# The low-part product of the attention logits over all 128 rows of the array

## The chip, the cores and the metric

The kernel runs on one core of a Trainium2 chip. The core has five engines that work side by side, each through its own instructions in order: TensorE (PE; its weight loads are shown apart as PEld), VectorE (DVE), ScalarE (ACT), GpSimd (POOL) and SyncE (SP), which here only issues DMAs. They share an on-chip memory of 128 partitions; PE writes into eight banks of a second memory (PSUM), which DVE and ACT read. The metric is the device time of one execution in microseconds (us).

## The reference, cut to what matters

One decoder block on 512 tokens of width 1024: a token-mixing half (attention with 8 heads of 64, beside a pooling branch) and a feed-forward half of width 2816. All in float32.

```
h = rms_norm(x) * (1 + scale1(c)) + shift1(c)
q, k, v, p, g_attn, g_pool = split(h @ W_in)
q, k = rms_norm(q per head), rms_norm(k per head)
logits = q k^T * 64^-0.5 + bias(distance), causal
attn = softmax(logits) v
pool = (trailing window mean of p - p) @ pool_w * pool_scale
merged = sigmoid(g_attn) * (attn @ Wa) + sigmoid(g_pool) * (pool @ Wp)
x = x + gate1(c) * (merged @ W_out)
u = causal_conv3((rms_norm(x) * (1 + scale2(c)) + shift2(c)) @ W_up)
x = x + gate2(c) * ((silu(u_g) * u_v) @ W_down)
```

With 512 tokens in blocks of 256, each query's own block and the one past block are all selected, so the block-sparse attention is plain causal attention.

## The kernel before

PE multiplies in a reduced form of float32 (fp32r). To keep accuracy each operand is split into a high part (rounded to that form) and a low part (what is left), and a product is made of three passes: high x high, high x low, low x high (`mm3`, lines 117 to 120). ACT makes most of the high parts, DVE the low parts.

The stages follow each other on PE: q and p projections while h is still being made, then k, then v, then eight heads of attention woven into the sixteen units of the two gate projections, then the branch merge, the output projection, the up projection with convolution, and the down projection. Weights come in units of 128x1024 (512 KB) by DMAs from SP, as many at a time as there are buffers (`wraw`, 5), two units ahead of their use (`ahead`, `unit`).

The order of PE, DVE and ACT is the order in which the code is written: generators (`tok_proj`, `gate_proj`) yield after each step of three passes, and `fill` (line 350) takes as many steps as a number of microseconds says before it lets the next piece of attention in. POOL takes the reciprocal square roots (`pow`), the low part of one q unit and of W_out, and issues the DMAs of the bias rows (`trev`).

The logits of a head have only 64 channels, half the array. So the two halves of the 128 partitions are put to use (`stacks`, from line 387): Q of a head is a tile of 128 rows whose one half holds the high part of q and whose other half the low part; K1 holds the high part of k in both halves. One 128-row product Q x K1 gives (q_hi + q_lo) k_hi. What is missing, q_hi k_lo, is a product over 64 rows, with K2: the low part of k in the same half in which Q holds q_hi. One tile K2 serves a pair of heads, the even head's low part in rows 0 to 63 and the odd head's in rows 64 to 127, and the low product reads one half of it and of Q:

```
K1[h], K2[h] = k1, k2[a]                                            # line 410
half = slice((h % 2) * 64, (h % 2) * 64 + 64)                       # line 422
nc.tensor.matmul(sps[:, :n], Q[h][half, tslice(qt)], K2[h][:, :n], start=True, stop=False)   # line 431
nc.tensor.matmul(sps[:, :n], Q[h][:, tslice(qt)], K1[h][:, :n], start=False, stop=True)      # line 432
```

`logits(h)` does so for four query tiles, the last first, over n = 512, 384, 256 and 256 keys: eight products, 64-row and 128-row in turn. DVE then adds the bias and takes the maximum of each row (line 440), ACT the exponential (line 444), DVE normalizes (line 454). `flip(h)` transposes the probabilities on PE (line 467), ACT and DVE split them, and `values(h)` multiplies by v (line 481); ACT copies half of the result (`bot`, line 488) and DVE adds (line 489). The loop over heads (lines 596 to 614) writes: flip(h), logits(h + 1), softmax(h + 1), some gate steps, the stacks of a later pair, values(h), a modulation column or two (`ada_col`, line 181), gate steps. Head 0's logits stand in the v projection (line 571). When a gate unit is done, ACT copies it out of its bank (line 347).

The tiles Q, K1, K2, the bias rows, probabilities and most others are slots of one pool of 72 (`slot`, line 66).

Of the kernel before, what the change touches and what calls it, by code (L numbers as in the profile page):

```python
# [7 lines left out]
F32 = mybir.dt.float32  # L8
F32R = mybir.dt.float32r
# [6 lines left out]
P = 128  # L16
# [10 lines left out]
BIG = 1e30  # L27
# [4 lines left out]
ET = mybir.EngineType  # L32
ENG = {ET.PE, ET.DVE, ET.Activation}

# columns of the constant pack
C_N1 = 0
C_N2 = C_N1 + 8
C_QG = C_N2 + 8
# [10 lines left out]
def block_kernel(tc, x, cvec, ada, wtok, wch, pool_w, wbr, wout, wup, wdn, pack, table, out):  # L49
    nc = tc.nc  # L50
# [3 lines left out]
    with ctx:  # L54
# [11 lines left out]
        def slot(name, dt=F32, w=512):  # L66
            return sp.tile([P, w], dt, tag="s", name=name)
# [6 lines left out]
            nc.sync.dma_start(raw, src)  # L74
            return raw

        # weight units in the order the tensor engine takes them
        plan = []
        for i in range(4):
            plan += [(wtok[12 + i], f"p{i}"), (wtok[i], f"q{i}")]  # L80
# [19 lines left out]
            return hi  # L100

        def ahead(name, n=2, on_dve=False, pool=()):
            """Emits loads and splits up to n units past the named one."""
            while upto[0] < min(len(plan), pos[name] + n + 1):
                src, nm = plan[upto[0]]
                raw = early.pop(nm) if nm in early else load_unit(src, nm)
                hi = his.pop(nm) if nm in his else hi_of(nm, raw, on_dve)
                lo = wlo_p.tile([P, 1024], F32R, tag="lo", name=f"lo_{nm}")
                (nc.gpsimd if nm in pool else nc.vector).tensor_sub(lo, raw, hi.bitcast(F32))  # L109
                ready[nm] = (hi, lo)  # L110
                upto[0] += 1
# [8 lines left out]
            nc.tensor.matmul(ps, sl, mh, start=False, stop=stop)  # L120

        def mm3s(ops, start, stop, late=0):
            """The three passes of several products, pass by pass; late: the moving low part comes last."""
            for ps, sh, sl, mh, ml in ops:
                nc.tensor.matmul(ps, sh, mh, start=start, stop=False)
            for i in ((1, 0) if late else (0, 1)):
                for ps, sh, sl, mh, ml in ops:
                    nc.tensor.matmul(ps, sl if i else sh, mh if i else ml, start=False, stop=stop and i != late)  # L128

        tslice = lambda t: slice(t * P, (t + 1) * P)  # L130

# [1 line left out]
        pk = cpool.tile([P, C_END], F32, name="pk")  # L133
        ident = pk[:, C_ID : C_ID + P]
        col = lambda i: pk[:, i : i + 1]
# [9 lines left out]
        nc.vector.memset(mhalf, -0.5)  # L145
        acol = cpool.tile([P, 48], F32, name="acol")

# [1 line left out]
        xt = []  # L149
        for t in range(TT):  # L150
            row = []
# [4 lines left out]
            xt.append(row)  # L156

        def rms_rows(tiles, name):
            """1 / rms per token of two [128, 512] halves of a token tile."""
            ss = mini.tile([P, 2], F32, tag="ss", name=f"ss_{name}")  # L160
            for f in range(2):
                junk = slot(f"junk_{name}_{f}")
                if f == 0:
                    nc.scalar.activation(junk, tiles[f], AF.Square, scale=1.0 / math.sqrt(D), accum_out=ss[:, f : f + 1])
                else:
                    nc.vector.tensor_tensor_reduce(
                        out=junk, in0=tiles[f], in1=tiles[f], op0=ALU.mult, op1=ALU.add, scale=1.0 / D,
                        scalar=EPS, accum_out=ss[:, f : f + 1])
            ms = mini.tile([P, 1], F32, tag="ms", name=f"ms_{name}")
            nc.vector.tensor_add(ms, ss[:, 0:1], ss[:, 1:2])  # L170
            rs = mini.tile([P, 1], F32, tag="rs", name=f"rs_{name}")
            nc.gpsimd.tensor_tensor(rs, ms, mhalf[:, 0:1], op=ALU.pow)
            return rs

# [1 line left out]
        def ada_load(g, k):  # L176
            return load_unit(ada[g * 8 + k], f"ada_{g * 8 + k}")

# [15 lines left out]
            (eng or nc.vector).tensor_sub(lo[:, :w], src, hi[:, :w].bitcast(F32))  # L194
            return hi, lo

# [1 line left out]
        fd = dpool.tile([H, NF], F32, name="fd")  # L198

        def bias_table():  # L200
# [38 lines left out]
            else:  # L239
                nc.vector.tensor_scalar(xs[k], xT[k], col(C_N1 + k), None, op0=ALU.mult)  # L240

        # loads of the first phase: modulation rows and weights, as many at a time as there are buffers
        queue = [(0, 0), (1, 0), "p0", "q0", (0, 1), (1, 1), (0, 2), (1, 2), "p1", "q1", (0, 3), (1, 3),
                 (0, 4), (1, 4), (0, 5), (1, 5), "p2", "q2", (0, 6), (1, 6), (0, 7), (1, 7), "p3", "q3"]
        held = [0]
# [30 lines left out]
        def lo_h(k):  # L276
            nc.vector.tensor_sub(hl[k], xs[k], hh[k].bitcast(F32))

# [1 line left out]
        pump()  # L280
        sum_h(0)
        gs = mini.tile([P, 1], F32, tag="gs", name="gs")
# [16 lines left out]
        for k in range(KT):  # L299
            i = k // 2  # L300
# [54 lines left out]
                us -= c  # L355

        def head_sums(ps, name):
            """1 / rms over each head's 64 columns of the token-major tiles."""
            res = []
            for t in range(TT):  # L360
                sq = slot(f"sq_{name}_{t}")
                nc.scalar.activation(sq, ps[t], AF.Square)
                ss = mini.tile([P, H], F32, tag="hs", name=f"hs_{name}_{t}")
                nc.vector.tensor_reduce(ss, sq.rearrange("p (h d) -> p h d", d=64), axis=AX.X, op=ALU.add)
                nc.vector.tensor_scalar(ss, ss, 1.0 / 64, EPS, op0=ALU.mult, op1=ALU.add)
                rs = mini.tile([P, H], F32, tag="hr", name=f"hr_{name}_{t}")
                nc.gpsimd.tensor_tensor(rs, ss, mhalf, op=ALU.pow)
                res.append(rs)
            return res
# [11 lines left out]
        qgn = cpool.tile([P, 1], F32, name="qgn")  # L381
        nc.vector.tensor_scalar(qgn, col(C_QG), -0.125, None, op0=ALU.mult)

# [1 line left out]
        Q, K1, K2 = {}, {}, {}  # L385

        def stacks(pr, isq):
            src, gain = (qn, qgn) if isq else (kn, col(C_KG))
            tp = bank(f"T_{pr}_{isq}")
            for t in range(TT):  # L390
                nc.tensor.transpose(tp[:, tslice(t)], src[t][:, tslice(pr)], ident)
            for e in range(2):
                h = 2 * pr + e
                a = slice(e * 64, e * 64 + 64)
                b = slice(64 - e * 64, 128 - e * 64)
                if isq:
                    q = slot(f"Q_{h}", F32R)
                    nc.scalar.activation(q[a], tp[a], AF.Copy, scale=gain[a])
                    nc.vector.scalar_tensor_tensor(
                        q[b], tp[a], gain[a], q[a].bitcast(F32), op0=ALU.mult, op1=ALU.subtract)  # L400
                    Q[h] = q
                else:
                    k1 = slot(f"K1_{h}", F32R)
                    if e == 0:
                        k2 = slot(f"K2_{pr}", F32R)
                    for r in (a, b):
                        nc.scalar.activation(k1[r], tp[a], AF.Copy, scale=gain[a])
                    nc.vector.scalar_tensor_tensor(
                        k2[a], tp[a], gain[a], k1[a].bitcast(F32), op0=ALU.mult, op1=ALU.subtract)
                    K1[h], K2[h] = k1, k2[a]  # L410

        ath, atl = [], []
        apair = {}

        def logits(h):
            """exp of head h's logits less their maximum: four query tiles over their causal keys."""
            trev = slot(f"trev_{h}")
            fsrc = fd[h : h + 1, :]
            nc.gpsimd.dma_start(
                trev, bass.AP(tensor=fsrc.tensor, offset=fsrc.offset, ap=[[1, P], [1, 512]]))  # L420
            ta = trev[:, :]
            half = slice((h % 2) * 64, (h % 2) * 64 + 64)
            pss = []
            for qt in (3, 2, 1, 0):
                n = max((qt + 1) * P, 256)
                if qt:
                    sb = bank(f"S_{h}_{qt}")
                    sps = sb
                else:
                    sps = sb[:, 256:]  # L430
                nc.tensor.matmul(sps[:, :n], Q[h][half, tslice(qt)], K2[h][:, :n], start=True, stop=False)  # L431
                nc.tensor.matmul(sps[:, :n], Q[h][:, tslice(qt)], K1[h][:, :n], start=False, stop=True)  # L432
                pss.append(sps)
            rows, sms = [], []
            for i, qt in enumerate((3, 2, 1, 0)):
                n = (qt + 1) * P
# [4 lines left out]
                    out=L[:, :n], in0=pss[i][:, :n], in1=rev, op0=ALU.add, op1=ALU.min, scale=1.0,  # L441
# [12 lines left out]
                nc.vector.tensor_scalar(rows[i][:, :n], rows[i][:, :n], ri, None, op0=ALU.mult)  # L454
            return rows[::-1]

        # P^T: key tile on the partitions; key tile kt holds queries kt*128 ..
        place = {0: (0, 0), 1: (1, 0), 3: (1, 384), 2: (2, 0)}

        def flip(h, rows):  # L460
# [31 lines left out]
                ath.append(a)  # L492
                atl.append(b)

# [1 line left out]
        plh, pll, pls = {}, {}, {}  # L496
        pwh = slot("pwh", F32R)
        pwl = slot("pwl", F32R)
# [25 lines left out]
                tl, ps2, col(C_PS + g), th.bitcast(F32), op0=ALU.mult, op1=ALU.subtract)  # L524
            plh[g], pll[g] = th, tl

# [1 line left out]
        praw = []  # L528
        for g in range(4):
            pt = slot(f"pt_{g}")  # L530
# [24 lines left out]
        fill(kgen, 2)  # L555
        fill(kgen, 100)

# [1 line left out]
        kr = head_sums(kps, "k")  # L559
        vps = [bank(f"v_{t}") for t in range(TT)]  # L560
        vgen = tok_proj(2, vps, "v")
# [9 lines left out]
        rows = logits(0)  # L571
        fill(vgen, 2)
        rows = softmax(0, *rows)
# [9 lines left out]
                nc.vector.tensor_sub(dst[:, :, 1], src, dst[:, :, 0].bitcast(F32))  # L583
            vst.append(vt)

# [1 line left out]
        gates = {}  # L587

        def gate_stream():
# [24 lines left out]
            fill(gg, (share - 3) / 2)  # L614
        fill(gg, 1000)

# [1 line left out]
        def row_of(g, name):  # L618
            rows = []
            for f in range(2):  # L620
# [36 lines left out]
            ada_col(4, k)  # L657
        late = [KT - 2, KT - 1]

# [1 line left out]
        wsel = lambda k, f: wo[(k // 2) * 4 + f * 2 + k % 2]  # L661
        x2, xr = [], {}
        h2h = [slot(f"h2h_{k}", F32R) for k in range(KT)]
# [63 lines left out]
                out_post(3, 0, ops[3, 0])  # L727
                flip_h2(1)

# [1 line left out]
        yh, yl = [], []  # L731

        def conv(ps, i, name):
# [41 lines left out]
            if 4 <= j < 12:  # L775
                ada_col(5, j - 4)

# [1 line left out]
        g2 = row_of(5, "g2")  # L779
        NK = NP // 2  # L780
        for f in range(2):
# [99 lines left out]
```

## Time and profile before

| | |
|---|---|
| median of 3 runs | 704.27 us (704.16 to 704.55) |
| span of the profiled execution, from first to last instruction | 702.0 us |
| what lies around the span (704.27 - 702.0) | 2.3 us |
| instructions in the profile | 8487 |
| DMA: 94.50 MB, mean | 135 GB/s |

The profile gives no separate time for the execution it was taken from; the median of the runs less its span is taken as what lies around it. Times in the profile's rows count from the span's start. In a timeline's row stand the start in us, the duration in us, the engine, the line, the operation, the tile written and the tiles read, the shapes, the count, and in brackets how long the engine had been idle and what ended that. For PE the shape 64*128 is the stationary operand (rows of the array by columns), and 64x512 the moving one (rows by columns). A PE row's duration reaches to a modelled end and overlaps the next row: distances are read from start to start. The tile names in rows leave the numbers out: S is a head's logits, PT its transposed probabilities, O its values product.

### The profile page before, as it was taken

How to read it: one execution, taken by the hardware profiler on the slowest of the kernel's cores; microseconds unless marked ns; L12 is line 12 of the kernel's file. 1: busy time of each engine (PE TensorE's matmuls, PEld its weight loads, DVE VectorE, ACT ScalarE, POOL GpSimd, SP SyncE). 2: the span in 40 equal slices, each digit the busy share in tenths (PEclk: the TensorE clock that was granted, in tenths of full speed). 3: DMA queues.
4: the chain of work that ended last, by engine and by line, in shares of the span. 5: the costliest groups of instructions: out<-in, count | busy, mean ns of one | idle time of the engine just before them, and what ended most of it. 6: DMA issues, size and time to landing. Idle time of an engine off the chain costs nothing.

```text
span 702.0 us, 8487 instructions
## 1 busy us (share of the span) xinstructions
PE 690.7 (98%) x3238; PEld 568.9 (81%) x3238; DVE 443.7 (63%) x719; ACT 304.8 (43%) x490; POOL 57.6 (8%) x56
## 2 busy tenths in 40 slices
PE   6999999999999999999999999999999999999997
PEld 4788787777777888888988888888888888888886
DVE  5795876776777598876576676776655653225213
ACT  6554447555554565504654343453443433122110
POOL 2103040000000045601000000000000000000000
PEclk9999999999999999999999999999999999999999
DMA  8785241544442356681123434534323233324001
GB/s 313 267 350 180 71 141 38 165 132 146 151 136 93 102 187 207 196 312 60 62 69 112 150 122 149 158 115 148 97 83 120 66 114 123 116 91 151 31 1 60
DMA packets 27631, 94.50 MB, mean 135 GB/s; under 512 B 3283, under 2 KB 3708, under 8 KB 27590
## 3 DMA queue, kind: packets, MB, share of 16 engines
q1 hardware_dynamic: 26198, 89.63, 37.7%
q0 software_dynamic: 1392, 4.33, 2.2%
q8 instruction: 25, 0.41, 0.2%
q14 instruction: 16, 0.13, 0.0%
HBM read 91.83 MB, written 2.12 MB: 134 GB/s over the span
## 4 chain that ended last, share of the span: by engine, by line
PE 95%; ACT 2%; DVE 1%; issue 1%; DMA 1%; SPq 0%; POOL 0%; DVEq 0%
PE u L118 11%; PE u L119 11%; PE u L120 11%; PE d L119 6%; PE d L118 6%; PE d L120 6%; PE gate_ps L120 4%; PE gate_ps L119 4%; PE gate_ps L118 4%; PE o L120 2%; PE o L118 2%; PE o L119 2%; PE S L432 2%; PE S L431 2%; PE O L481 1%; PE p L128 1%
## 5 line engine op out<-in xcount | busy, mean ns | idle before, releaser
L118 PE MATMUL u<-h2h,hi_up 128*128 128x512 f32 (+1 forms) x384 | 142.7, 372 | 0.0
L119 PE MATMUL u<-h2l,hi_up 128*128 128x512 f32 (+1 forms) x384 | 142.6, 371 | 0.0
L120 PE MATMUL u<-h2h,lo_up 128*128 128x512 f32 (+1 forms) x384 | 142.6, 371 | 0.0
L120 PEld LDWEIGHTS u<-h2h,lo_up 128*128 128x128 f32 x384 | 72.3, 188 | 12.6
L118 PEld LDWEIGHTS u<-h2h,hi_up 128*128 128x128 f32 x384 | 72.3, 188 | 12.5
L119 PEld LDWEIGHTS u<-h2l,hi_up 128*128 128x128 f32 x384 | 72.3, 188 | 12.3
L118 PE MATMUL d<-hi_dn,y_h 128*128 128x512 f32 (+1 forms) x198 | 72.6, 367 | 0.0
L119 PE MATMUL d<-lo_dn,y_h 128*128 128x512 f32 (+1 forms) x198 | 72.6, 367 | 0.0
L120 PE MATMUL d<-hi_dn,y_l 128*128 128x512 f32 (+1 forms) x198 | 72.4, 365 | 0.0
L109 DVE TENSOR_TENSOR lo_dn<-raw_dn,hi_dn 128x1024 fp32r<-128x1024 f32 x22 | 26.6, 1224 | 61.6 <-ACT hi_dn L99 61.6
L181 DVE CUSTOM_DVE_ANT_0 raw_ada<-raw_ada,cbc 128x1026 f32<-128x1026 f32 x48 | 61.1, 1293 | 3.0 <-DMA raw_ada<-in_ada 3.0
L109 DVE TENSOR_TENSOR lo_up<-raw_up,hi_up 128x1024 fp32r<-128x1024 f32 x44 | 52.1, 1221 | 8.6 <-ACT hi_up L99 8.6
L99 ACT ACTIVATE hi_dn<-raw_dn 128x1024 fp32r<-128x1024 f32 x22 | 23.0, 1059 | 75.0 <-PE d L120 61.7
L736 ACT ACTIVATE uv<-u,pk 128x512 f32<-128x512 f32 x22 | 17.2, 780 | 87.1 <-PE u L120 87.1
L120 PE MATMUL gate_ps<-h_h,lo_gate 128*128 128x512 f32 x128 | 50.0, 390 | 0.0
L119 PE MATMUL gate_ps<-h_l,hi_gate 128*128 128x512 f32 x128 | 49.9, 390 | 0.0
L118 PE MATMUL gate_ps<-h_h,hi_gate 128*128 128x512 f32 x128 | 49.9, 390 | 0.0
L737 DVE SCALAR_TENSOR_TENSOR uv<-u,pk,uv 128x511 f32<-128x511 f32 x22 | 16.5, 749 | 52.5 <-ACT uv L736 52.5
L99 ACT ACTIVATE hi_up<-raw_up 128x1024 fp32r<-128x1024 f32 x44 | 44.1, 1046 | 4.3 <-PE u L119 4.3
L118 PEld LDWEIGHTS d<-hi_dn,y_h 128*128 128x128 f32 x198 | 37.4, 189 | 6.3
L119 PEld LDWEIGHTS d<-lo_dn,y_h 128*128 128x128 f32 x198 | 37.3, 189 | 6.1
L120 PEld LDWEIGHTS d<-hi_dn,y_l 128*128 128x128 f32 x198 | 37.3, 188 | 6.1
(201 smaller groups left out, 1241.0 us busy)
## 6 DMA issues: line engine op xcount, KB each, us to landing
raw_ada<-in_ada SPq DMA_DIRECT2D x48, 513.0 KB, 4.8
raw_up<-in_wup SPq DMA_DIRECT2D x44, 512.0 KB, 4.3
raw_dn<-in_wdn SPq DMA_DIRECT2D x22, 512.0 KB, 3.4
raw_gate<-in_wch SPq DMA_DIRECT2D x16, 512.0 KB, 5.3
raw_br<-in_wbr SPq DMA_DIRECT2D x8, 512.0 KB, 3.8
raw_wo<-in_wout SPq DMA_DIRECT2D x8, 512.0 KB, 3.2
x<-in_x SPq DMA_DIRECT2D x8, 256.0 KB, 4.4
raw_p<-in_wtok SPq DMA_DIRECT2D x4, 512.0 KB, 5.9
```

What stands on the lines that cost most here:

```text
L99: nc.scalar.activation(hi, raw, AF.Copy)
L109: (nc.gpsimd if nm in pool else nc.vector).tensor_sub(lo, raw, hi.bitcast(F32))
L118: nc.tensor.matmul(ps, sh, mh, start=start, stop=False)
L119: nc.tensor.matmul(ps, sh, ml, start=False, stop=False)
L120: nc.tensor.matmul(ps, sl, mh, start=False, stop=stop)
L128: nc.tensor.matmul(ps, sl if i else sh, mh if i else ml, start=False, stop=stop and i != late)
L181: nc.vector.tensor_tensor_reduce(out=raw, in0=raw, in1=cbc, op0=ALU.mult, op1=ALU.add, scale=1.0, scalar=0.0, accum_out=acol[:, i : i + 1])
L431: nc.tensor.matmul(sps[:, :n], Q[h][half, tslice(qt)], K2[h][:, :n], start=True, stop=False)
L432: nc.tensor.matmul(sps[:, :n], Q[h][:, tslice(qt)], K1[h][:, :n], start=False, stop=True)
L481: nc.tensor.matmul(ops[:, kt * P :], lw, m[b_][:, o : o + w], start=(i == 0 and j == 0), stop=(i == 3 and j == 1))
L736: nc.scalar.activation(t, ps, AF.Identity, scale=cw(2), bias=col(C_CB + i))
L737: nc.vector.scalar_tensor_tensor(t[:, 1:], ps[:, : S - 1], cw(1), t[:, 1:], op0=ALU.mult, op1=ALU.add)
```

## The change

The low part of k gets a tile with all 128 rows: the 64 rows that hold the low part, and zeros in the other 64. The low product then reads all of Q and all of that tile; the rows of Q that hold q_lo meet zeros, so the sum is the same.

The zeros are written once: four tiles `kz` (even and odd head, and two pairs in turn) are taken from the slots before the k projection, and POOL sets the half of each that the low part does not use to zero. `stacks` writes the low part of a head into the other half of `kz[e, pr % 2]`; no K2 tile is taken. In the loop, DVE's write for pair pr + 2 goes to the tile that pair pr used.

```
@@ stacks and what stands ahead of it @@
         Q, K1, K2 = {}, {}, {}
+        kz = {}
+        for e in range(2):
+            for i in range(2):
+                z = slot(f"kz_{e}_{i}", F32R)
+                nc.gpsimd.memset(z[64 - e * 64 : 128 - e * 64].bitcast(F32), 0.0)
+                kz[e, i] = z
...
                     k1 = slot(f"K1_{h}", F32R)
-                    if e == 0:
-                        k2 = slot(f"K2_{pr}", F32R)
+                    k2 = kz[e, pr % 2]
...
-                    K1[h], K2[h] = k1, k2[a]
+                    K1[h], K2[h] = k1, k2
@@ logits @@
-            half = slice((h % 2) * 64, (h % 2) * 64 + 64)
...
-                nc.tensor.matmul(sps[:, :n], Q[h][half, tslice(qt)], K2[h][:, :n], start=True, stop=False)
+                nc.tensor.matmul(sps[:, :n], Q[h][:, tslice(qt)], K2[h][:, :n], start=True, stop=False)
```

Besides, comments and docstrings are dropped, and lines behind the new loop stand four further down.

The order on PE does not change. This is PE from the end of head 0's transposes to the first gate product behind head 1's logits, before (S_1_3 is head 1, query tile 3; K2_0 the low parts of pair 0; K1_1 the high part of head 1):

```order
L467 MATMUL PT_0_2_1152<-pk_80,L_0_3_1012 128x128
L431 MATMUL S_1_3_1161<-K2_0_958,Q_1_920 128x512 [waits DVE_49,PE_49]
L432 MATMUL S_1_3_1161<-K1_1_962,Q_1_920 128x512
L431 MATMUL S_1_2_1164<-K2_0_958,Q_1_920 128x384 [waits DVE_49,PE_49]
L432 MATMUL S_1_2_1164<-K1_1_962,Q_1_920 128x384
L431 MATMUL S_1_1_1167<-K2_0_958,Q_1_920 128x256 [waits DVE_49,PE_49]
L432 MATMUL S_1_1_1167<-K1_1_962,Q_1_920 128x256
```

And the same place in the changed kernel (the shape at a row's end is that of the output; the row count of the operands is not shown):

```order
L471 MATMUL PT_0_2_1159<-pk_80,L_0_3_1019 128x128
L435 MATMUL S_1_3_1168<-kz_1_0_578,Q_1_928 128x512 [waits DVE_49,PE_49,Pool_49]
L436 MATMUL S_1_3_1168<-K1_1_969,Q_1_928 128x512
L435 MATMUL S_1_2_1171<-kz_1_0_578,Q_1_928 128x384 [waits DVE_49,PE_49]
L436 MATMUL S_1_2_1171<-K1_1_969,Q_1_928 128x384
L435 MATMUL S_1_1_1174<-kz_1_0_578,Q_1_928 128x256 [waits DVE_49,PE_49]
L436 MATMUL S_1_1_1174<-K1_1_969,Q_1_928 128x256
```

Nothing moved; the low product reads kz (odd head, first of the two) in place of K2, and the first of the block waits for POOL too, which wrote the zeros.

On POOL the four memsets stand between the low part of a q unit and the four `pow` of q's norm. Before:

```order
L109 TENSOR_TENSOR lo_q1_299<-raw_q1_249,hi_q1_297 128x1024 [waits DMAHW3_49,Activation_49]
L367 TENSOR_TENSOR hr_q_0_589<-hs_q_0_586,mhalf_89 128x8 [waits DVE_49]
L367 TENSOR_TENSOR hr_q_1_596<-hs_q_1_593,mhalf_89 128x8 [waits DVE_49]
L367 TENSOR_TENSOR hr_q_2_603<-hs_q_2_600,mhalf_89 128x8 [waits DVE_49]
L367 TENSOR_TENSOR hr_q_3_610<-hs_q_3_607,mhalf_89 128x8 [waits DVE_49]
```

And in the changed kernel:

```order
L109 TENSOR_TENSOR lo_q1_299<-raw_q1_249,hi_q1_297 128x1024 [waits DMAHW3_49,Activation_49]
L390 MEMSET kz_0_0_574 64x512 [waits Pool_49]
L390 MEMSET kz_0_1_576 64x512
L390 MEMSET kz_1_0_578 64x512
L390 MEMSET kz_1_1_580 64x512
L367 TENSOR_TENSOR hr_q_0_597<-hs_q_0_594,mhalf_89 128x8 [waits DVE_49,Pool_49]
```

Four instructions came in, waiting for nothing but POOL itself; what stood behind them follows in the same order.

## The prediction

> **What bounds the kernel now.** I read the page first, then the busy time of the stage that the change touches, then that stage's matmuls and weight loads one by one.
>
> ```profile
> span 702.0 us, 8487 instructions
> PE 690.7 (98%) x3238; PEld 568.9 (81%) x3238; DVE 443.7 (63%) x719; ACT 304.8 (43%) x490; POOL 57.6 (8%) x56
> PE 95%; ACT 2%; DVE 1%; issue 1%; DMA 1%; SPq 0%; POOL 0%; DVEq 0%
> ```
>
> TensorE is busy for 98% of the span, and the chain that ended last is 95% TensorE. So a microsecond taken from TensorE comes off the end, as long as nobody becomes late behind it. The second view is the busy time of each engine between 106 and 235 us, the stretch that holds the eight logits blocks (columns: length, then busy us and instruction count of PE, weight load, DVE, ACT, POOL, then clock, DMA share, GB/s).
>
> ```profile
> 106.00:235.00 129.00, 129.00 (x596) 101.12 (x595) 95.61 (x232) 74.36 (x155) 3.29 (x6) 1.00 0.38 120
> ```
>
> PE never stops there, at full granted clock. DVE is busy for 95.61 of 129 us (74%), ACT for 58%, and DMA moves 120 GB/s at a share of 0.38. There is room, though DVE's is not boundless.
>
> "Busy" hides something, because the end of a matmul is modelled: what counts is the distance from start to start. These are head 0's logits on PE (start, duration, line, tiles, rows*columns of the stationary side, moving shape):
>
> ```profile
> 106.13 0.39 PE L120 MATMUL v<-hi_v,h_l 128*128 128x512 f32 x1
> 106.45 0.50 PE L431 MATMUL S<-K,Q 64*128 64x512 f32 x1
> 106.87 0.49 PE L432 MATMUL S<-K,Q 128*128 128x512 f32 x1
> 107.30 0.44 PE L431 MATMUL S<-K,Q 64*128 64x384 f32 x1
> 107.67 0.44 PE L432 MATMUL S<-K,Q 128*128 128x384 f32 x1
> 108.04 0.38 PE L431 MATMUL S<-K,Q 64*128 64x256 f32 x1
> 108.35 0.38 PE L432 MATMUL S<-K,Q 128*128 128x256 f32 x1
> 108.66 0.38 PE L431 MATMUL S<-K,Q 64*128 64x256 f32 x1
> 108.98 0.38 PE L432 MATMUL S<-K,Q 128*128 128x256 f32 x1
> 109.20 0.40 PE L118 MATMUL v<-hi_v,h_h 128*128 128x512 f32 x1
> ```
>
> Start to start the two 512-column products take 0.42 and 0.43, the 384-column ones 0.37 each, the 256-column ones 0.31, 0.31, 0.32 and 0.22. The block is 2.75 us long (106.45 to 109.20), and the step into it is 0.32. A 64-row product takes as long as the 128-row one of the same width (0.50 and 0.49, 0.44 and 0.44, 0.38 and 0.38): the half array saves nothing.
>
> The weight loads beside them say where the time goes:
>
> ```profile
> 105.90 0.19 PEld L120 LDWEIGHTS v<-hi_v,h_l 128*128 128x128 f32 x1
> 106.44 0.18 PEld L431 LDWEIGHTS S<-K,Q 64*128 64x128 f32 x1 [0.35 <-issue]
> 106.87 0.19 PEld L432 LDWEIGHTS S<-K,Q 128*128 128x128 f32 x1 [0.24 <-issue]
> 109.08 0.19 PEld L118 LDWEIGHTS v<-hi_v,h_h 128*128 128x128 f32 x1
> ```
>
> In the v stream the load for the matmul at 106.13 starts at 105.90, 0.23 us ahead, beside the matmul before. In the logits block a load starts together with its own matmul (106.44 and 106.45, 106.87 and 106.87): it was not brought forward, and the array waits for it. The idle time is put down to "issue", not to an engine. All eight blocks are alike; the last one runs from 223.77 to 226.52, again 2.75:
>
> ```profile
> 223.77 0.49 PE L431 MATMUL S<-K,Q 64*128 64x512 f32 x1
> 224.63 0.43 PE L431 MATMUL S<-K,Q 64*128 64x384 f32 x1
> 226.52 0.40 PE L118 MATMUL gate_ps<-h_h,hi_gate 128*128 128x512 f32 x1
> ```
>
> Is it the change of row count that keeps the load back? The kernel holds one other place where it changes: the bias table's products (33 rows, 8 columns) between k products.
>
> ```profile
> 77.84 1.24 PE L203 MATMUL fp<-hot,rel 33*8 33x512 f32 x4
> 79.01 0.19 PEld L118 LDWEIGHTS k<-hi_k,h_h 128*128 128x128 f32 x1 [0.22 <-issue]
> 79.12 0.19 PEld L119 LDWEIGHTS k<-lo_k,h_h 128*128 128x128 f32 x1
> ```
>
> Here too the first load of the other shape stands idle for 0.22 with "issue" as the reason, and the next, of the same shape, follows 0.11 behind. These products share no operand with their neighbours, so a common tile isn't what holds the load.
>
> **The change part by part.** The low product of every query tile now takes 128 rows on both sides. Counts, widths and order of the 64 logits matmuls stay. Per block there were eight switches of row count, one on the way in and seven inside. All go.
>
> What does the block take without them? The step into it becomes an ordinary 512-column step; inside, the widths go at the rates that 128-row streams show elsewhere. A stretch of the values product gives 512 and 384 columns, one of the up projection 256:
>
> ```profile
> 213.35 0.39 PE L481 MATMUL O<-PT_l,v 128*128 128x512 f32 x1
> 213.58 0.33 PE L481 MATMUL O<-PT_h,v 128*128 128x384 f32 x1
> 213.75 0.34 PE L481 MATMUL O<-PT_l,v 128*128 128x384 f32 x1
> 213.93 0.22 PE L481 MATMUL O<-PT_h,v 128*128 128x128 f32 x1
> ...
> 344.78 0.28 PE L119 MATMUL u<-h2l,hi_up 128*128 128x256 f32 x1
> 344.90 0.28 PE L120 MATMUL u<-h2h,lo_up 128*128 128x256 f32 x1
> ```
>
> That is 0.23, 0.17 to 0.18, and 0.12. The block: 2 x 0.23 + 2 x 0.175 + 4 x 0.12 = 1.29 us in place of 2.75, and the step into it 0.23 in place of 0.32. Per head 1.46 + 0.09 = 1.55 us; for eight heads **12.4 us off PE**. From both sides: were all 2816 columns streamed at 0.23 per 512, a block would be 1.27, so 0.2 us more in all; if the loads stay late, nothing goes. I take the 12.4, since three streams of this kernel show these steps.
>
> One rule weighs against this. The Trainium skill's page "TensorE: Matmul & The Clock Gate", Part 3, says under "What overlaps and what doesn't" that a weight load overlaps a running matmul only when its row group differs; by it a full-row load behind a full-row matmul has to wait, and the change would gain nothing. The row at 105.90 speaks against it: full rows on both sides, and loaded 0.23 ahead.
>
> Does anybody fall behind? Each block's 1.55 us is time that DVE and ACT had. The tight place I find is the last block: its second low product (224.63) writes a bank that ACT's copy of a gate product must have emptied, and that copy stands behind a DVE chain that starts at head 5's sum.
>
> ```profile
> 215.28 0.69 DVE L489 TENSOR_TENSOR at<-O,bot 64x512 f32<-64x512 f32 x1 [0.93 <-ACT bot L488]
> ...
> 223.28 0.60 ACT L347 ACTIVATE gate<-gate_ps 128x512 f32<-128x512 f32 x1
> ```
>
> The copy ends at 223.88, 0.75 before 224.63. With the block of the head before shorter by 1.55, its values product and ACT's `bot` come 1.55 earlier, but DVE has only 0.93 of waiting to give up there, so the chain ends 0.62 later relative to PE. The waiting product itself comes another 0.09 + (0.86 - 0.46) = 0.49 earlier in its own block. 0.75 - 0.62 - 0.49 = -0.36: a **new wait of about 0.4 us**. Its ends are none and 1.3 (the chain not moving at all: 0.75 - 1.55 - 0.49).
>
> The added part: four 64x512 memsets on POOL, queued behind the q split and ahead of q's power function. No row shows one of that size. The ends are the 128x1 memset (0.10 us) and the two-input 128x512 subtraction (1.62), so 0.4 to 6.5 us for four, on an idle queue:
>
> ```profile
> L870 POOL MEMSET const-float32-0.0<- 128x1 f32 x1 | 0.1, 99 | 0.2 <-issue 0.2
> ...
> L194 POOL TENSOR_TENSOR wo_l<-raw_wo,wo_h 128x512 fp32r<-128x512 f32 x16 | 25.6, 1624 | 55.1 <-ACT wo_h L193 55.1
> ...
> 28.27 2.49 POOL L109 TENSOR_TENSOR lo_q<-raw_q,hi_q 128x1024 fp32r<-128x1024 f32 x1 [16.29 <-ACT hi_q L99]
> 63.23 6.96 POOL L367 TENSOR_TENSOR hr_q<-hs_q,mhalf 128x8 f32<-128x8 f32 x4 [32.47 <-DVE hs_q L365]
> ```
>
> POOL is idle from 30.76 to 63.23, so they are done long before q's norm and before the first logits at 106, which now wait for POOL as well; cost on the queue nothing. But POOL can hold up DVE: beside the q split a DVE sum took 3.42 us and ended 1.07 after it, and PE waited 0.91 for the h that hangs on these sums:
>
> ```profile
> 28.41 3.42 DVE L181 CUSTOM_DVE_ANT_0 raw_ada<-raw_ada,cbc 128x1026 f32<-128x1026 f32 x1
> ...
> 34.56 1.20 PE L125 MATMUL p<-h_h,hi_p 128*128 128x512 f32 x4 [0.91 <-ACT h_h L272]
> ```
>
> If the memsets do the same, up to 6.5 us go onto the path. I take 0, nearer to the small memset, since a memset has no operand to read. The Trainium skill's "SBUF — State Buffer", "SBUF: two separate sides", has a DVE operation with two inputs blocked only by a GpSimd operation that reads SBUF; by it the price is 0 too, and no run yet shows it.
>
> DVE's writes keep their number, shape and place; they go to the shared pair of zero tiles, whose readers are two pairs of heads back. Four slots are held for longer, which changes which slot the bias rows take, but these are issued early: head 3's at 145.18 for a use at 156.81, and two shorter blocks take 3.1 of these 11.6 us.
>
> ```profile
> 145.18 0.55 POOL L419 DMA_DIRECT2D trev<-fd  x1 [23.66 <-PE O L481]
> ...
> 156.81 0.68 DVE L440 CUSTOM_DVE_ANT_0 L<-S,trev 128x512 f32<-128x512 f32 x1
> ```
>
> The sum: -12.4 + 0.4 = -12.0 us. The profiled execution's span is 702.0; the times have a median of 704.27, so 2.3 lie around the span. 702.0 - 12.0 + 2.3 = **692.3 us**, 1.7% less.
>
> **The rivals.**
>
> *Waits take part of it.* DVE works in order and would be 82% busy in the shorter stage (95.61 of 129 - 12.4 = 116.6 us). If the 0.62 found in one head came onto PE in each of the seven heads after the first, 4.4 us would be lost: 696.7. Against it: PE has no gap in this stage now, and where DVE waits (0.93 in the row above) it waits for work that PE sets off, so it mostly moves along with PE. 10%, 692.7 to 696.7.
>
> *The memsets hold DVE.* 0.4 to 6.5 us back: 692.7 to 698.8. Their place is where PE is already waiting. 4%.
>
> *The change doesn't do what it says.* The load is held by something else: a load for all rows might not run beside a product on all rows, or the tile Q, from which both products of a pair load, might hold it. PE's steps stay, 704.3. The v stream speaks against the first, the bias-table rows against the second. 4%.
>
> *Slower.* The loads stay late and the memsets sit on the path at 34.56: 704.3 plus 0.4 to 6.5, so 704.7 to 710.8. It decides only if the blocks give back less than the memsets take, that is, stay above 2.75 - 6.5 / 8 = 1.94 us. 3%.
>
> **How the numbers follow.** Forecast 79%, 692.3, by itself 691.3 to 693.2: no new wait (-0.4), the streaming end (-0.2) and the rows' rounding to 0.01 (some 0.05 per block, 0.4) below; a wait of 1.3 in place of 0.4 above. The range reaches over the first rival: 691.3 to 696.7. A measurement of this kernel can tell about 0.2% (1.4 us) from no change: faster by more 93%, within it 4%, slower 3%.
>
> **What would show it.** In the changed kernel's trace a logits load starts beside the matmul before it, 0.12 to 0.23 ahead of its own; a block runs 1.3 us from its first start to the next product; "issue" is gone as its reason; PE is still without gaps from 106 to the end of the gates except a few tenths in the last block; and h's matmul near 34.56 waits no longer than 0.91. Blocks of 2.75 would make the prediction wrong at its first step; blocks of 1.3 with gaps elsewhere would leave the first step and overturn the second.

## The result, and the profile after

| | before | after |
|---|---|---|
| median (runs measured together) | 704.21 us (703.92 to 704.55, 4 runs) | 691.46 us (691.40 to 691.90, 4 runs) |
| span of the profiled execution | 702.0 us | 689.6 us |

The ratio is 0.9821, with a 95% interval from 0.9807 to 0.9835: 1.8% faster. The forecast was 692.3 us, with a range from 691.3 to 696.7. The span fell by 12.4 us.

The page of the changed kernel begins with the span, the busy time and, further down, the chain that ended last:

```profile
span 689.6 us, 8494 instructions
PE 677.6 (98%) x3238; PEld 566.5 (82%) x3238; DVE 443.2 (64%) x719; ACT 304.4 (44%) x490; POOL 59.4 (9%) x60
PE 94%; DMA 2%; ACT 1%; DVE 1%; SPq 1%; issue 1%; DVEq 0%; ACTq 0%
```

PE has as many matmuls and loads as before (3238 each) and is busy for 677.6 in place of 690.7 us; DVE and ACT hardly moved, POOL took 1.8 us more. PE is still the bound.

The stage of the logits blocks, by the busy time of each engine (the columns are those of the row shown before, here from 106 to 222.5):

```profile
106.00:222.50 116.50, 116.50 (x596) 99.29 (x595) 92.77 (x228) 73.14 (x154) 3.28 (x6) 1.00 0.41 132
```

The same 596 matmuls that took 129.00 us now take 116.50, with no gap: what PE gave up was not filled by a wait for DVE, which now works 92.77 of 116.5 us (80%).

Head 0's block on PE, instruction by instruction:

```profile
106.16 0.39 PE L120 MATMUL v<-hi_v,h_l 128*128 128x512 f32 x1
106.39 0.39 PE L435 MATMUL S<-kz,Q 128*128 128x512 f32 x1
106.61 0.39 PE L436 MATMUL S<-K,Q 128*128 128x512 f32 x1
106.84 0.33 PE L435 MATMUL S<-kz,Q 128*128 128x384 f32 x1
107.01 0.34 PE L436 MATMUL S<-K,Q 128*128 128x384 f32 x1
107.19 0.28 PE L435 MATMUL S<-kz,Q 128*128 128x256 f32 x1
107.30 0.28 PE L436 MATMUL S<-K,Q 128*128 128x256 f32 x1
107.42 0.28 PE L435 MATMUL S<-kz,Q 128*128 128x256 f32 x1
107.54 0.29 PE L436 MATMUL S<-K,Q 128*128 128x256 f32 x1
107.67 0.40 PE L118 MATMUL v<-hi_v,h_h 128*128 128x512 f32 x1
```

Start to start the step into the block is 0.23, the block itself 1.28 (106.39 to 107.67): 512 columns in 0.22 to 0.23, 384 in 0.17 to 0.18, 256 in 0.11 to 0.13. The loads beside them:

```profile
106.16 0.19 PEld L435 LDWEIGHTS S<-kz,Q 128*128 128x128 f32 x1
106.39 0.19 PEld L436 LDWEIGHTS S<-K,Q 128*128 128x128 f32 x1
```

The load for the product at 106.39 starts at 106.16, together with the matmul before it, and so does the next one. In this block "issue" is gone as a reason.

### The profile page after: what moved, and what is told of

The parts are those of the page before. It is cut to its first block, busy times and chain, and to the rows that moved or that the text cites. A ratio compares the mean times of both kernels' runs of the same rounds, so it can differ in the third digit from the quotient of the medians.

```text
span 689.6 us, 8494 instructions
## 1 busy us (share of the span) xinstructions
PE 677.6 (98%) x3238; PEld 566.5 (82%) x3238; DVE 443.2 (64%) x719; ACT 304.4 (44%) x490; POOL 59.4 (9%) x60
## 4 chain that ended last, share of the span: by engine, by line
PE 94%; DMA 2%; ACT 1%; DVE 1%; SPq 1%; issue 1%; DVEq 0%; ACTq 0%
PE u L119 12%; PE u L120 12%; PE u L118 12%; PE d L118 6%; PE d L119 6%; PE d L120 6%; PE gate_ps L120 4%; PE gate_ps L119 4%; PE gate_ps L118 4%; PE o L118 2%; PE o L119 2%; PE o L120 2%; DMA raw_ada<-in_ada 2%; PE O L485 2%; PE p L128 1%; PE q L128 1%
## 5 line engine op out<-in xcount | busy, mean ns | idle before, releaser
L119 PEld LDWEIGHTS u<-h2l,hi_up 128*128 128x128 f32 x384 | 72.3, 188 | 12.5
```

Source lines behind the costliest of these rows:

```text
L119: nc.tensor.matmul(ps, sh, ml, start=False, stop=False)
```

## The experiments

Seven kernels were timed against the kernel before; three more have one execution and its trace each, and one of these was then timed too. In the table "switches" are changes between 64 and 128 rows from one PE product to the next, over the eight logits blocks. Each ratio is to the kernel before as measured together with that run (medians from 703.91 to 704.21 us).

| run | 64-row products | switches | median, us | ratio to before (95%) |
|---|---|---|---|---|
| kernel before | 32 | 64 | 704.21 | 1 |
| 64-row slices of the zero tiles | 32 | 64 | 703.98 | 0.9999 (0.9989 to 1.0008) |
| another order, six switches a block | 32 | 48 | 701.08 | 0.9957 (0.9942 to 0.9971) |
| pairs, four switches a block | 32 | 32 | 697.98 | 0.9912 (0.9895 to 0.9928) |
| two low products of four on 64 rows | 16 | 32 | 697.95 | 0.9915 (0.9900 to 0.9930) |
| the changed kernel | 0 | 0 | 691.46 | 0.9821 (0.9807 to 0.9835) |
| the changed kernel in the pairs' order | 0 | 0 | 691.59 | 0.9821 (0.9806 to 0.9836) |

The time follows the switches and not the number of 64-row products. Against 691.46 a switch costs 6.5 / 32 = 0.20, 9.6 / 48 = 0.20 and 12.5 / 64 = 0.20 us.

**The 64-row products in pairs.** From the kernel before; lines 431 and 432 become:

```
+                two = [(Q[h][half, tslice(qt)], K2[h]), (Q[h][:, tslice(qt)], K1[h])]
+                for j, (w, m) in enumerate(two[::-1] if qt in (3, 1) else two):
+                    nc.tensor.matmul(sps[:, :n], w, m[:, :n], start=j == 0, stop=j == 1)
```

> The kernel before with its 64-row low products kept, but put in neighbouring pairs (order of a block: high 3, low 3, low 2, high 2, high 1, low 1, low 0, high 0): as many 64-row products as before, four changes of row count per block in place of eight. Theory A (each change of row count between neighbouring products costs 12.4 / 64 = 0.194 us): half of the gain, 704.2 - 4 x 8 x 0.194 = 698.0 us; inside a pair the second low product's load starts beside the first product. Rival B (each 64-row product costs 0.39 us, whatever stands beside it): 704.2 us. Rival C (it is the zero tiles' place or the slots, not the product's rows): 704.2 us.

Measured: 697.98 us, ratio 0.9912 (0.9895 to 0.9928). Theory A's 698.0 is inside, B's and C's 704.2 (a ratio of 1) outside. The loads of a pair in head 0's block:

```profile
107.37 0.18 PEld L433 LDWEIGHTS S<-K,Q 64*128 64x128 f32 x1 [0.35 <-issue]
107.48 0.19 PEld L433 LDWEIGHTS S<-K,Q 64*128 64x128 f32 x1
107.97 0.19 PEld L433 LDWEIGHTS S<-K,Q 128*128 128x128 f32 x1 [0.30 <-issue]
```

and the products that belong to the first two:

```profile
107.37 0.49 PE L433 MATMUL S<-K,Q 64*128 64x512 f32 x1
107.71 0.33 PE L433 MATMUL S<-K,Q 64*128 64x384 f32 x1
```

The first 64-row load comes late, together with its product at 107.37. The second, 64 rows behind 64 rows, starts at 107.48, 0.23 ahead of its product at 107.71. The next one, on 128 rows, is late again. So it isn't a 64-row product that costs, but its neighbour of another size.

**Six switches.** The same edit with `qt in (2, 0)`.

> The kernel before with another order (low 3, high 3, high 2, low 2, low 1, high 1, high 0, low 0): as many 64-row products, six changes of row count per block in place of eight. Theory A (0.194 us per change): 704.2 - 2 x 8 x 0.194 = 701.1 us. Rivals B (a price per 64-row product) and C (tiles or slots): 704.2 us.

Measured: 701.08 us, ratio 0.9957 (0.9942 to 0.9971). A's 701.1 was met; the loss is proportional to the number of switches.

**The order by itself.** The edit of the pairs, made to the changed kernel (both products on `Q[h][:, tslice(qt)]`).

> Control for the order: the changed kernel, all products on 128 rows, in the order of the run with pairs. Theory A: no change of row count, 691.5 us. If the order by itself moved the time (earlier or later ends of the tiles that the softmax reads), it would differ from 691.5 by as much as the run with pairs differs from its forecast.

Measured: 691.59 us, ratio 0.9821 (0.9806 to 0.9836). The order is worth nothing that shows, so the 698 of the pairs is due to the rows.

**The zero tiles kept, 64 rows read.** From the changed kernel:

```
-                nc.tensor.matmul(sps[:, :n], Q[h][:, tslice(qt)], K2[h][:, :n], start=True, stop=False)
+                half = slice((h % 2) * 64, (h % 2) * 64 + 64)
+                rw = half if True else slice(0, P)
+                nc.tensor.matmul(sps[:, :n], Q[h][rw, tslice(qt)], K2[h][rw, :n], start=True, stop=False)
```

> The changed kernel with its zero tiles, memsets and slots, but its low products read only the 64 rows that hold data. Theory A, and B alike: all of the gain goes, 704.0 us, with the loads starting together with their own product again. Rival C (the tiles, the slots or the memsets brought the gain): 691.5 us.

Measured: 703.98 us, ratio 0.9999 (0.9989 to 1.0008). All of the gain is gone with the tiles, the memsets and the slots in place: rival C falls. In head 0's block the loads start together with their own products again (106.84 and 106.85, 107.27 and 107.27).

**Half of the low products on 64 rows.** The same edit for query tiles 3 and 1 alone: `if qt in (3, 1)` stands in place of `if True`.

> The changed kernel, in which the low products of query tiles 3 and 1 read 64 rows again and those of 2 and 0 read 128: two 64-row products and four changes of row count per block. Theory A: 691.5 + 4 x 8 x 0.194 = 697.7 us. B gives the same here (2 x 8 x 0.39 = 6.2); a price that only the first switch of a block pays, or one that grows with the width of the product, would miss it.

Measured: 697.95 us, ratio 0.9915 (0.9900 to 0.9930), where 697.7 was forecast. A price that only the first switch of a block pays, or one that grows with the width, is excluded; rival B gives the same here and fell with the pairs. Its block shows where the 0.2 us of a switch lies:

```profile
106.13 0.39 PE L120 MATMUL v<-hi_v,h_l 128*128 128x512 f32 x1
106.45 0.50 PE L437 MATMUL S<-kz,Q 64*128 64x512 f32 x1
106.88 0.50 PE L438 MATMUL S<-K,Q 128*128 128x512 f32 x1
107.21 0.33 PE L437 MATMUL S<-kz,Q 128*128 128x384 f32 x1
107.38 0.34 PE L438 MATMUL S<-K,Q 128*128 128x384 f32 x1
107.65 0.38 PE L437 MATMUL S<-kz,Q 64*128 64x256 f32 x1
107.96 0.39 PE L438 MATMUL S<-K,Q 128*128 128x256 f32 x1
108.18 0.28 PE L437 MATMUL S<-kz,Q 128*128 128x256 f32 x1
```

The step 106.13 to 106.45, with a switch at its end, is 0.32, which is 0.09 above the 0.23 of a 512-column step. The step 106.88 to 107.21, with a switch at its start, is 0.33, 0.10 above. The step between them has a switch at both ends: 0.43, 0.20 above. The 256-column step from 107.96, with a switch at its start, is 0.22 in place of 0.12. So in these blocks a switch delays the product that it leads to by 0.09 us, and the one behind that by another 0.10, from 512 to 256 columns.

**Which change of rows is a switch?** The prediction said any change of row count. From the changed kernel:

```
-                nc.tensor.matmul(sps[:, :n], Q[h][:, tslice(qt)], K2[h][:, :n], start=True, stop=False)
+                rw = slice(0, 128 if h % 2 else 96)
+                nc.tensor.matmul(sps[:, :n], Q[h][rw, tslice(qt)], K2[h][rw, :n], start=True, stop=False)
```

> The changed kernel, in which the even heads' low products read 96 rows (64 of data, 32 of zeros) and the odd heads' 128. If any change of row count costs, as the prediction put it: 4 heads x 8 x 0.194 = 6.2 us, 697.7 us. If only a change between sizes of a part of the array costs, and 96 rows take the whole array as 128 do: 691.5 us, with each load beside the product before it.

Measured: 691.68 us, ratio 0.9822 (0.9806 to 0.9839). Head 0's loads and products:

```profile
106.56 0.19 PEld L436 LDWEIGHTS S<-kz,Q 96*128 96x128 f32 x1
106.78 0.19 PEld L437 LDWEIGHTS S<-K,Q 128*128 128x128 f32 x1
```

```profile
106.78 0.40 PE L436 MATMUL S<-kz,Q 96*128 96x512 f32 x1
107.01 0.40 PE L437 MATMUL S<-K,Q 128*128 128x512 f32 x1
107.25 0.34 PE L436 MATMUL S<-kz,Q 96*128 96x384 f32 x1
```

The row count changes from 128 to 96 and back at every step, each load starts one step ahead, and the steps are 0.23 and 0.24. It is not the number of rows that has to be equal: 64 beside 128 costs, 96 beside 128 doesn't.

**Rows or columns?** The prediction's second evidence, the bias table's products on 33 rows and 8 columns, differs from its neighbours in both. Three versions of the changed kernel pad them with zeros, with three memsets more on POOL:

```
+        for t in (rb_, hot[0], hot[1]):
+            nc.gpsimd.memset(t, 0.0)
...
-                nc.tensor.matmul(fp[:H, :n], rb_[: NB + 1, :H], hot[i][: NB + 1, :n], start=True, stop=True)
+                nc.tensor.matmul(fp[:H, :n], rb_[:P, :H], hot[i][:P, :n], start=True, stop=True)
```

This one is 128 rows by 8 columns; the second takes `rb_[: NB + 1, :P]` (33 by 128), the third `rb_[:P, :P]` (128 by 128), both with the output `fp[:P, :n]`.

> The changed kernel with the bias table's four products padded with zeros from 33 rows and 8 columns of the stationary side to 128 rows and 8 columns. Read at the products, not in the time (the most that can go is some 0.3 us). Theory A (it is the row count): the first k load behind them starts beside the matmul before it and its idle time of 0.22 with issue as its reason is gone. Rival (it is the column count): that idle time stays.

> The changed kernel with the bias table's four products padded with zeros from 33 rows and 8 columns to 33 rows and 128 columns. Theory A (row count): the idle time of 0.22 ahead of the first k load behind them stays. Rival (column count): it goes.

> The changed kernel with the bias table's four products padded with zeros to 128 rows and 128 columns, after padding of rows alone (steps in, 0.318, and out, 0.202 + 0.341) and of columns alone (0.318; 0.202 + 0.335) had left both switches. If a switch is any difference in size, of rows or columns, it goes now: a step of 0.23 after them in place of 0.34, some 0.2 us at the way out, the way in still waiting for DVE or not; the time 691.1 to 691.5 us. If these products pay for something else (their wait for DVE), the steps stay.

The products around the place in the version with 128 rows and 8 columns:

```profile
77.65 0.39 PE L120 MATMUL k<-hi_k,h_l 128*128 128x512 f32 x1
77.97 1.24 PE L203 MATMUL fp<-hot,rel 128*8 128x512 f32 x4
79.14 0.50 PE L118 MATMUL k<-hi_k,h_h 128*128 128x512 f32 x1
79.48 0.40 PE L119 MATMUL k<-lo_k,h_h 128*128 128x512 f32 x1
```

in that with 33 rows and 128 columns:

```profile
77.68 0.39 PE L120 MATMUL k<-hi_k,h_l 128*128 128x512 f32 x1
78.00 1.34 PE L203 MATMUL fp<-hot,rel 33*128 33x512 f32 x4
79.27 0.50 PE L118 MATMUL k<-hi_k,h_h 128*128 128x512 f32 x1
79.61 0.40 PE L119 MATMUL k<-lo_k,h_h 128*128 128x512 f32 x1
```

and in that with 128 of both:

```profile
77.38 0.39 PE L120 MATMUL k<-hi_k,h_l 128*128 128x512 f32 x1
77.61 1.24 PE L203 MATMUL fp<-hot,rel 128*128 128x512 f32 x4
78.61 0.47 PE L118 MATMUL k<-hi_k,h_h 128*128 128x512 f32 x1
78.92 0.39 PE L119 MATMUL k<-lo_k,h_h 128*128 128x512 f32 x1
```

and there the load of the first k product behind the group:

```profile
78.58 0.19 PEld L118 LDWEIGHTS k<-hi_k,h_h 128*128 128x128 f32 x1
```

With 128 rows and 8 columns nothing was gained: 0.32 into the group and 0.34 behind the first k product, where a 512-column step takes 0.23, so theory A's forecast for this run was wrong. With 33 rows and 128 columns the 0.34 stays too, as A said. Only with both equal does the step in fall to 0.23, and the stretch from 77.38 to 78.92 takes 1.54 us, where it took 1.83 (77.65 to 79.48) with 8 columns. On the way out the gain lies elsewhere than the expectation had it: the step behind the first k product is still 0.31 and not 0.23, but this product now starts 0.03 behind the last of the group (78.58 to 78.61), where that step was 0.20 with 8 columns. So a difference in either rows or columns makes a switch, and one in both costs no more: the changed kernel, with 33 rows and 8 columns, takes the same 1.83 us (77.55 to 79.38 in its trace). With 33 rows and 128 columns the stretch is 1.93 (77.68 to 79.61): the second product of the group comes 0.53 behind the first, where it is 0.43 in the versions with 8 columns and in that with 128 of both. The second part of a switch, the 0.10 us, thus didn't show behind the way in to 8-column operands, whose load takes 0.09 us in place of 0.19.

The rival that these products wait for DVE can be read off as well. The profile puts the idle time ahead of their first load down to DVE's norm of q (line 377). With 128 rows and 8 columns that load starts 2.22 us after the norm's start (75.75 to 77.97); in the later execution of the version with 128 of both it starts 1.91 after it (75.82 to 77.73). So DVE was ready earlier than the late load, and it wasn't DVE that held it.

The single times were 691.55, 691.69 and 690.93 us. The last was timed again:

> The kernel of the run before this one again (the bias table's products padded to 128 rows and 128 columns), timed in five rounds: its trace had 0.29 us less between the k products on both sides of the bias table. If that reaches the end: 691.2 us, a ratio of 0.9817 to the kernel before, which an interval of about 0.001 can't tell from the changed kernel's 0.9821. If padding costs elsewhere (three memsets more on POOL): above 691.5 us.

Measured: 691.24 us (691.13 to 691.51), ratio 0.9819 (0.9806 to 0.9832). Its median is 0.2 us below the changed kernel's and the intervals overlap, so the trace's 0.29 us is not confirmed as a gain in the time. The trace of this later execution repeats the stretch of 1.54 us (77.72 to 79.26).

**The memsets.** From the changed kernel, each memset five times:

```
+                for _ in range(5):
+                    nc.gpsimd.memset(z[64 - e * 64 : 128 - e * 64].bitcast(F32), 0.0)
```

> The changed kernel with each of the four memsets issued five times (20 of 0.52 us, some 10 us of POOL from 30.9 us on, beside DVE's sums before PE's wait near 34.6). If memsets don't hold DVE up: 691.5 us and a wait of 0.91 near 34.6 as before. Rival (a memset holds a DVE operation with two inputs for as long as it runs): up to 8 us more, 692 to 699.5, with DVE's sums after 31 us several us longer.

Measured: 691.59 us, ratio 0.9824 (0.9808 to 0.9841). POOL was at it from 31.17 to 41.56:

```profile
28.62 2.49 POOL L109 TENSOR_TENSOR lo_q<-raw_q,hi_q 128x1024 fp32r<-128x1024 f32 x1 [16.59 <-ACT hi_q L99]
31.17 10.39 POOL L391 MEMSET kz<- 64x512 f32 x20
```

while DVE went on beside it:

```profile
28.77 3.43 DVE L181 CUSTOM_DVE_ANT_0 raw_ada<-raw_ada,cbc 128x1026 f32<-128x1026 f32 x1
32.13 1.22 DVE L181 CUSTOM_DVE_ANT_0 raw_ada<-raw_ada,cbc 128x1026 f32<-128x1026 f32 x1
34.90 0.69 DVE L277 TENSOR_TENSOR h_l<-xs,h_h 128x512 fp32r<-128x512 f32 x1 [1.55 <-ACT h_h L272]
```

Each memset is 0.52 us (10.39 / 20). Beside them the sum at 32.13 takes 1.22 us and the subtraction 0.69; the same sum beside the two-input subtraction on POOL takes 3.43. In one detail the expectation missed: PE's wait for h was not near 34.6 in this execution but earlier, once, and 1.3 us long; in the changed kernel there were two, of 1.6 and 0.9. DVE's subtraction for h starts 6.13 us behind the stretched sum here (28.77 to 34.90) and 6.12 in the changed kernel (28.46 to 34.58), so the memsets put nothing between them, and the median is 0.1 us above the changed kernel's.

## Why the prediction was right

*The eight switches of a block (-12.4 us).* Right in mechanism and size. Head 0's block was forecast at 1.29 us with a step of 0.23 into it, and took 1.28 and 0.23. The blocks behind a head's ten transposes are split differently. This is the last one:

```profile
211.75 1.25 PE L471 MATMUL PT<-pk,L 128*128 128x128 f32 x10
212.76 0.48 PE L435 MATMUL S<-kz,Q 128*128 128x512 f32 x1
213.08 0.40 PE L436 MATMUL S<-K,Q 128*128 128x512 f32 x1
213.31 0.34 PE L435 MATMUL S<-kz,Q 128*128 128x384 f32 x1
...
214.14 0.40 PE L118 MATMUL gate_ps<-h_h,hi_gate 128*128 128x512 f32 x1
```

Its first product takes a step of 0.32 behind the transposes, so the block is 1.38 us long, but it starts 1.01 us behind the transposes' first start, where that was 1.19 before (222.58 to 223.77). From their first start to the gate product it is 2.39 us. Before it was 3.94, by the one row that is missing among those shown:

```profile
222.58 1.26 PE L467 MATMUL PT<-pk,L 128*128 128x128 f32 x10
```

(222.58 to 226.52). So 1.55 us are saved here as well. In each of the eight blocks it is 1.54 to 1.56, and 8 x 1.55 = 12.4. That the two profiled spans differ by just as much is in part luck, since spans of the kernel before lay between 701.7 and 702.8 us; the medians differ by 12.75.

*Its reason, "a change of row count".* Too wide in one way and too narrow in another. The runs show that a change between 64 and 128 rows costs 0.2 us and one between 96 and 128 nothing, and that a change of columns from 128 to 8 is a switch too. The bias-table rows supported the right conclusion, though they couldn't tell rows from columns. The Trainium skill's page "TensorEngine Tiling (Array Packing)" says under "Key Properties" that a change of the tiling mode drains TensorE, and lists under "Available Configurations" modes of 128, 64 and 32 rows and of 128, 64 and 32 columns. The runs agree in that 64 beside 128 rows and 8 beside 128 columns cost; that the array drains then isn't seen as such, only that a load starts no earlier than its own product. The rule on weight loads that the prediction cites from the Trainium skill's page "TensorE: Matmul & The Clock Gate" would have the change gain nothing; it doesn't hold here, for the load at 106.16 runs beside a product on the same 128 rows. Whether other sizes (32 rows, 64 columns) are switches among themselves wasn't tried.

*The new wait in the last block (+0.4 us).* Wrong: it didn't come. The step that failed is the sentence that this block's second low product waits for ACT's copy of the gate product that ended at 223.88. In the changed kernel that product starts at 213.31, in the fence above, and ACT's copies beside it are these:

```profile
202.28 0.58 ACT L347 ACTIVATE gate<-gate_ps 128x512 f32<-128x512 f32 x1
...
213.15 0.60 ACT L347 ACTIVATE gate<-gate_ps 128x512 f32<-128x512 f32 x1
```

The product starts while the copy from 213.15 to 213.75 is still running, so it can't be waiting for it. Its load does wait for ACT by its semaphore, but the last gate copy that can have emptied its bank is the one before, which ended at 202.86, over ten us earlier. The lag of the later copy was sized well: it ended 1.30 us behind the transposes' first start before (222.58 to 223.88) and 2.00 behind it now (211.75 to 213.75), 0.70 later where 0.62 was forecast. But it is the lag of a copy that no product of the block waits for.

*Memsets (0).* Right: 0.52 us each in place of the bounds 0.1 and 1.62, and five times as many moved neither DVE nor the time. The sum of 2.0 us on POOL lies in its idle time.

*Outside the span (2.3 us).* Too large. Later executions have time and span on record together: 691.40 with 689.6 in the changed kernel, 704.22 with 702.4 in the one with the 64-row slices. That is 1.8 us; 2.3 came from subtracting the span of one execution from the median of others. The miss of 692.3 - 691.5 = 0.8 us is the wait (a span of 690.0 in place of 689.6) and this (2.3 in place of 691.46 - 689.6 = 1.9).

*The rivals.* Waits did not take part of the gain: the eight blocks gave 12.4 us, and neither the span (12.4) nor the medians (12.75) fell by less. The memsets held nobody. That the load would stay late was excluded by the first trace, and slower needed both. The measured time is 0.2 us above the low end of the range.

## What to carry to other kernels

Where a PE stage shows loads that start together with their own matmul and "issue" as the reason, compare the sizes of neighbouring stationary operands: each change between 64 and 128 rows cost 0.2 us here, and a 64-row product was no shorter than a 128-row one. Padding with zeros removes it, and where zeros cost too much, an order that puts products of one size side by side gets half of it for no memory at all. Before a wait is added to a forecast, find out which instance of a repeated line writes the buffer that the waiting instruction takes; a bank that goes round has several.

## What the runs showed of the hardware that was not expected

A switch between 64 and 128 rows is paid in two parts, 0.09 us ahead of the product and 0.10 ahead of the one behind it, whatever the width (512 to 256 columns). Behind the way in to operands of 8 columns the second part didn't show (0.43 us between the first two products, against 0.53 with 128 columns). A product on 96 rows is no switch beside 128. One on 128 rows with 8 columns is, beside 128 columns, and so is one on 33 rows with 128 columns.
